# Casts in rows of 2 KB, rope tables loaded a unit ahead, and wide softmax sums, in an encoder layer on eight cores

## The chip, the cores and the metric

The kernel runs on the 8 cores of one Trainium2 chip, every core on its own half of one of the four batch items' queries. The metric is the device time of the slowest core, in microseconds (us). Engines are named as the profile names them: PE is TensorE (its weight loads, PEld, lie beside the matmuls), DVE is VectorE, ACT is ScalarE, POOL is GpSimd, SP is SyncE, which here only starts transfers.

An execution can fall in a slow state, in which one die's cores get a lower clock and the program takes some per cent longer.

## The reference, cut to what matters

```python
# per layer, x: (4, 4096, 2048) float32
qa, ka, va, qb, kb, vb, ga, gb = jnp.split(x @ w_in, split_pts, axis=-1)
qa = rope(rms_norm(qa))          # A: 8 query heads, 2 key heads, full softmax over 4096 keys
ka = rope(rms_norm(ka))
out_a = softmax(qa @ ka.T * scale) @ va
out_b = dilated_window_attention(qb, kb, vb)     # B: 12 heads in 3 groups of dilation 1, 4, 16
mixed = (sigmoid(ga + b0) * (out_a @ w_proj_a) + sigmoid(gb + b1) * (out_b @ w_proj_b)) @ w_out
x = layer_norm(ALPHA * x + mixed)
x = layer_norm(ALPHA * x + (silu(x @ w_ffn_gate) * (x @ w_ffn_up)) @ w_ffn_down)
```

The weights come as float32; the matmuls run in bfloat16. So each weight is cast once, either on its way into SBUF or, for out-projection and feed-forward weights that are read several times, from DRAM to a bfloat16 copy in DRAM.

## The kernel before

Instructions are recorded by a helper `s` that works out semaphores from the buffers read (`r`) and written (`w`); so in a profile nearly all matmuls carry one line number (L223), all two-input VectorE and GpSimd operations another (L232), and one reads by buffer names. SP starts loads and stores on the hardware queue (q1 in the profile). GpSimd starts transfers that cast, on the software queue (q0).

The casts of the later weights are a list of jobs, taken one or two at a time at chosen places of the program. Each is one transfer of 1 or 2 MB (counted as written), whose rows are 4 to 16 KB long.

```python
    jobs = []
    for j in range(22):
        jobs.append((wgb_d[j], w_fg_d[j], ("wgb", j)))
        jobs.append((wub_d[j], w_fu_d[j], ("wub", j)))
        jobs.append((wdb_d[j * 256:(j + 1) * 256, :], w_fd_d[j * 256:(j + 1) * 256, :], ("wdb", j)))
    for fb in range(4):
        jobs.append((wob_d[fb], w_out_d[fb], ("wob", fb)))
    jobs.reverse()
    ...
    def precast(n=1):
        for _ in range(min(n, len(jobs))):
            out, in_, key = jobs.pop()
            s.dma("pool", DMA(out, in_), w=[key])
```

The table of cosines and sines for 512 positions (512 KB) is loaded when the unit that needs it begins. There are two buffers:

```python
    def load_cs(tb):
        i = n_cs[0] % 2
        n_cs[0] += 1
        s.dma("sp", DMA(CS[i][:, :, :], rope_d[tb]), w=[(CS[i],)])
        return i
```

In `rope`, VectorE multiplies the projection by this table (R1, R2), and then makes SQL, the low half of the squares, which TensorE sums with a matrix of ones. That is why a late table shows up as TensorE waiting for SQL.

Attention A goes through 512 steps: 8 heads, 4 blocks of 512 queries, 16 steps of 256 keys. A group is the 16 steps of one head and block. A step is two score matmuls into one of three double banks, an exp on ScalarE (PT), and three steps later (LAG) two value matmuls. The sums of the softmax are built from pairs on VectorE and accumulated in float32 on GpSimd:

```python
            j = i - LAG
            if 0 <= j < len(steps):
                h, qb, pc = steps[j]
                g = h // 4
                p, q = PT[j % 6], PS[j % 6]
                s.dve(TT(q[:, :], p[:, 0:512], p[:, 512:1024], ALU.add), r=[(p,)], w=[(q,)])
                if pc % 2 == 1:
                    q0 = PS[(j - 1) % 6]
                    s.dve(TT(q[:, :], q[:, :], q0[:, :], ALU.add), r=[(q,), (q0,)], w=[(q,)])
                if pc == 3:
                    q1 = PS[(j - 2) % 6]
                    s.pool(TT(DAC[:, :], q[:, :], q1[:, :], ALU.add), r=[(q,), (q1,)], w=[(DAC,)])
                elif pc % 2 == 1 and pc > 3:
                    s.pool(TT(DAC[:, :], DAC[:, :], q[:, :], ALU.add), r=[(q,), (DAC,)], w=[(DAC,)])
                # ... value matmuls of step j into bank 6 ...
                if pc == 15:
                    ou = OU[(h * 4 + qb) % 2]
                    s.dve(CP(ou[:, :], psb[6][:, :]), w=[(ou,)], ps=[6])
                    s.pool(CP(DHI[:, :], DAC[:, :]), r=[(DAC,)], w=[(DHI,)])
                    s.pool(TT(DLO[:, :], DAC[:, :], DHI[:, :], ALU.subtract), r=[(DAC,), (DHI,)], w=[(DLO,)])
                    due.append((i + 5, h, qb))
            if due and i >= due[0][0]:
                # ... two ones-products (DHI, DLO) into bank 7 sum over the partitions ...
                s.dve(CP(rd[:, :], psb[7][:, :]), w=[(rd,)], ps=[7])
                s.dve(RECIP(rd[:, :], rd[:, :]), r=[(rd,)], w=[(rd,)])
                s.dve(TT(oa[:, :], ou[:, :], rd[:, :], ALU.mult), r=[(rd,), (ou,)], w=[(oa,)])
                s.dma("sp", DMA(oaT_d[h][:, qb * 512:(qb + 1) * 512], oa[:, :]), r=[(oa,)], w=[("oaT", h, qb)])
```

Between these steps TensorE also does the gate and projection of out_b ("fill"), whose results go to DRAM (mb). The keys of B (kbT) and queries of B are projected partly before and partly within attention B: each 512-column piece goes through one of four staging buffers STG to DRAM, and attention B loads them into KB and QB.

The softmax here doesn't subtract the row's maximum and nothing guards it: scores larger than these inputs give would overflow.

Of the kernel before, what the change touches and what calls it, by code (L numbers as in the profile page):

```python
# [5 lines left out]
F32 = mybir.dt.float32  # L6
# [275 lines left out]
def build_program():  # L282
# [86 lines left out]
    jobs = []  # L369
    for j in range(22):  # L370
        jobs.append((wgb_d[j], w_fg_d[j], ("wgb", j)))
        jobs.append((wub_d[j], w_fu_d[j], ("wub", j)))
        jobs.append((wdb_d[j * 256:(j + 1) * 256, :], w_fd_d[j * 256:(j + 1) * 256, :], ("wdb", j)))
    for fb in range(4):
        jobs.append((wob_d[fb], w_out_d[fb], ("wob", fb)))
# [88 lines left out]

    def load_cs(tb):
        i = n_cs[0] % 2
        n_cs[0] += 1
        s.dma("sp", DMA(CS[i][:, :, :], rope_d[tb]), w=[(CS[i],)])
        return i
# [147 lines left out]
    def vb_rest():  # L617
        load_r(5)
        for g in (1, 2):
            for i in range(2 if g == 1 else 0, B_TILES[g]):  # L620
                vb_tile(g, i)
                if i % 4 == 3:
                    precast()
                yield
            if g == 1:
                load_r(7)
        for i in range(6, 12):
            load_r(i + 3)
            for _ in kq_units(i, P1):
                yield  # L630
            precast(2)
# [155 lines left out]
    def kq_rest():  # L787
        for i in range(12, 18):
            load_r(i + 3)
            yield from kq_units(i, FB)  # L790
            precast(2)
# [24 lines left out]
    PT = [at("PT", [128, 1024], BF16, kb(120 + 2 * i)) for i in range(6)]  # L816
    PS = [at("PS", [128, 512], BF16, kb(132 + i)) for i in range(6)]
    DAC = at("DAC", [128, 512], F32, kb(138))
    DHI = at("DHI", [128, 512], BF16, kb(140))
    DLO = at("DLO", [128, 512], BF16, kb(141))  # L820
    RD = [at("RD", [128, 512], F32, kb(142 + 2 * i)) for i in range(2)]
    OU = [at("OU", [128, 512], F32, kb(146 + 2 * i)) for i in range(2)]
    OA = [at("OA", [128, 512], BF16, kb(150 + i)) for i in range(2)]
    OB = at("outbT", [128, 4, T], BF16, kb(96))
    MBL = [at("MBL", [128, T], F32, kb(152 + 8 * i)) for i in range(3)]
# [5 lines left out]
    FILL = {9: 2, 10: 1, 11: 2, 12: 1, 13: 2, 14: 2, 15: 1, 0: 2, 1: 1, 2: 2, 4: 2, 5: 2}  # L831

    def attn_a(fill):
# [3 lines left out]
        due = []  # L837
        load_kv(1)
        for i in range(len(steps) + LAG + 16):
            if i < len(steps):  # L840
                h, qb, pc = steps[i]
                g = h // 4
                if qb == 0 and pc == 0 and h + 1 < 8:
                    load_q(h + 1)
                bk = i % 3
                for e2 in range(2):
                    c = 2 * pc + e2
                    kf = FRAG[g * 4 + c // 8]
                    s.pe(MM(pbig[bk][:, e2 * 512:(e2 + 1) * 512], kf[:, (c % 8) * 128:(c % 8 + 1) * 128],
                            QT[h % 2][:, qb * 512:(qb + 1) * 512]),  # L850
                         r=[(kf,), (QT[h % 2],)], ps=[2 * bk + e2])
                s.act(ACTF(PT[i % 6][:, :], pbig[bk][:, :], AF.Exp), w=[(PT[i % 6],)], ps=[2 * bk, 2 * bk + 1])
# [6 lines left out]
            for _ in range(FILL.get(i % 16, 0) if i >= 16 + 9 else 0):  # L859
                next(fill, None)  # L860
            j = i - LAG
            if 0 <= j < len(steps):
                h, qb, pc = steps[j]
                g = h // 4
                p, q = PT[j % 6], PS[j % 6]
                s.dve(TT(q[:, :], p[:, 0:512], p[:, 512:1024], ALU.add), r=[(p,)], w=[(q,)])
                if pc % 2 == 1:
                    q0 = PS[(j - 1) % 6]
                    s.dve(TT(q[:, :], q[:, :], q0[:, :], ALU.add), r=[(q,), (q0,)], w=[(q,)])
                if pc == 3:  # L870
                    q1 = PS[(j - 2) % 6]
                    s.pool(TT(DAC[:, :], q[:, :], q1[:, :], ALU.add), r=[(q,), (q1,)], w=[(DAC,)])
                elif pc % 2 == 1 and pc > 3:
                    s.pool(TT(DAC[:, :], DAC[:, :], q[:, :], ALU.add), r=[(q,), (DAC,)], w=[(DAC,)])
                for jj in ((), (j - 1, j), (j,))[min(pc, 2)]:
                    pp = PT[jj % 6]
                    for e2 in range(2):
                        c = 2 * (jj % 16) + e2
                        vf = FRAG[8 + g * 4 + c // 8]
                        s.pe(MM(psb[6][:, :], vf[:, (c % 8) * 128:(c % 8 + 1) * 128], pp[:, e2 * 512:(e2 + 1) * 512],  # L880
                                start=(c == 0), stop=(c == 31)),
                             r=[(vf,), (pp,)], ps=[6])
                if pc == 15:
                    ou = OU[(h * 4 + qb) % 2]
                    s.dve(CP(ou[:, :], psb[6][:, :]), w=[(ou,)], ps=[6])
                    s.pool(CP(DHI[:, :], DAC[:, :]), r=[(DAC,)], w=[(DHI,)])
                    s.pool(TT(DLO[:, :], DAC[:, :], DHI[:, :], ALU.subtract), r=[(DAC,), (DHI,)], w=[(DLO,)])
                    due.append((i + 5, h, qb))
            if due and i >= due[0][0]:
                assert i % 16 == 7  # L890
                _, h, qb = due.pop(0)
                n = h * 4 + qb
                ou, oa, rd = OU[n % 2], OA[n % 2], RD[n % 2]
                s.pe(MM(psb[7][:, :], ones_b[:, :], DHI[:, :], start=True, stop=False), r=[(DHI,)], ps=[7])
                s.pe(MM(psb[7][:, :], ones_b[:, :], DLO[:, :], start=False, stop=True), r=[(DLO,)], ps=[7])
# [49 lines left out]
    def mb_fill():  # L945
        for f in range(NMB):
            for tb in range(4):
                t, st = TG[tb % 2], TG[2 + tb % 2]
                for kc, _ in enumerate(gate(f, 1, tb, 7)):
                    if kc == 15:  # L950
                        tanh(f, 1, 7, t)
                        precast(1 + (n_jobs() > NMB * 4 - f * 4 - tb))
# [6 lines left out]
            if f < 3:  # L959
                load_mb(f)  # L960
# [15 lines left out]
    load_oa(range(4, 8))  # L976
    MIX = [at("mixT", [128, T], BF16, kb(112 + 4 * f)) for f in range(16)]
# [28 lines left out]
    for f in range(16):  # L1006
# [8 lines left out]
        elif f == 14:  # L1015
            WO0A = at("WO0A", [128, 8, 512], BF16, kb(176))
            s.dma("sp", DMA(WO0A[:, :, :], wob_d[0][:, 0:4096].rearrange("p (k c) -> p k c", c=512)),
                  r=[("wob", 0)], w=[(WO0A,)])
# [15 lines left out]
    def load_wo(fb):  # L1034
        s.dma("sp", DMA(WO[fb][:, :, :], wob_d[fb].rearrange("p (k c) -> p k c", c=512)), r=[("wob", fb)], w=[(WO[fb],)])
# [58 lines left out]
    def next_bank():  # L1094
# [4 lines left out]
          r=[("wob", 0)], w=[(WO0B,)])  # L1099
# [42 lines left out]
    def ensure_gu(upto):  # L1142
        while gu_next[0] <= upto and gu_next[0] < 88:
# [3 lines left out]
            s.dma("sp", DMA(t[:, 0, :], wgb_d[i % 22]), r=[("wgb", i % 22)], w=[(t, 0)])  # L1147
            s.dma("sp", DMA(t[:, 1, :], wub_d[i % 22]), r=[("wub", i % 22)], w=[(t, 1)])

    def ensure_d(upto):  # L1150
        while d_next[0] <= upto and d_next[0] < 7 * NHC:
# [6 lines left out]
                  r=[("wdb", hc // 2)], w=[(t,)])  # L1158
# [60 lines left out]
    for tb in range(4):  # L1219
# [31 lines left out]
        for half in range(2):  # L1251
# [13 lines left out]
            for hc in range(NHC - 4):  # L1265
                ensure_d(d0 + hc + 7)
                if tb == 3:
                    t = WDL[hc]
                    s.dma("sp", DMA(t[:, :], wdb_d[hc * 128:(hc + 1) * 128, 1024:2048]), r=[("wdb", hc // 2)], w=[(t,)])
# [17 lines left out]
    for i, hc in enumerate(range(NHC - 4, NHC)):  # L1287
        t = WD[i]
        s.dma("sp", DMA(t[:, :], wdb_d[hc * 128:(hc + 1) * 128, 1024:2048]), r=[("wdb", hc // 2)], w=[(t,)])
# [117 lines left out]
```

## Time and profile before

Three runs took 4632 to 4638 us, and the cores agree within 1%. The stages below are read off TensorE's timeline at the first matmul of each kind (core 1, the slowest).

| stage | what it is | us |
|---|---|---|
| keys/values | keys and values of A, first value tiles of B | 289.9 |
| queries and keys | queries of A, value tiles of B; then keys and queries of B | 597.6 |
| attention B | first to last; other keys and queries of B woven in | 394.5 |
| attention A | first score matmul to last | 747.0 |
| to out-projection | the end of attention A and the mixing | 505.9 |
| rest | out-projection, norms, feed-forward | 2104.3 |

How to read it: a stage is worth shortening only by what TensorE stands still in it.

### The profile page before, as it was taken

How to read it: one execution, taken by the hardware profiler on the slowest of the kernel's cores; microseconds unless marked ns; L12 is line 12 of the kernel's file. 1: busy time of each engine (PE TensorE's matmuls, PEld its weight loads, DVE VectorE, ACT ScalarE, POOL GpSimd, SP SyncE). 2: the span in 40 equal slices, each digit the busy share in tenths (PEclk: the TensorE clock that was granted, in tenths of full speed). 3: DMA queues.
4: the chain of work that ended last, by engine and by line, in shares of the span. 5: the costliest groups of instructions: out<-in, count | busy, mean ns of one | idle time of the engine just before them, and what ended most of it. 6: DMA issues, size and time to landing. Idle time of an engine off the chain costs nothing.

```text
span 4639.1 us, 55832 instructions; the slowest of 8 cores (4603.6 to 4639.1 us)
## 1 busy us (share of the span) xinstructions
PE 4172.2 (90%) x19488; PEld 1930.7 (42%) x19488; DVE 1589.8 (34%) x2127; ACT 1079.1 (23%) x1432; POOL 448.1 (10%) x523
## 2 busy tenths in 40 slices
PE   6678598859788888879999999999999999999998
PEld 3333254324433333334444444444444444444443
DVE  1224230013688989962222661000220022012203
ACT  1223121112376666641111221000110011001100
POOL 2000000000034444420000000000000000000000
PEclk9889799989789999989999999999999999999999
DMA  9665748692455444363222456455455644554463
GB/s 158 107 97 91 110 84 136 136 150 103 159 102 94 97 96 84 64 112 92 45 38 83 174 179 212 170 176 166 169 198 166 178 173 178 170 170 170 175 191 111
DMA packets 233970, 622.24 MB, mean 134 GB/s; under 512 B 55328, under 2 KB 110624, under 8 KB 200224
## 3 DMA queue, kind: packets, MB, share of 16 engines
q1 hardware_dynamic: 197808, 476.01, 31.7%
q0 software_dynamic: 35888, 142.65, 21.0%
q8 instruction: 162, 2.65, 0.2%
q14 instruction: 112, 0.92, 0.1%
HBM read 676.61 MB, written 162.20 MB: 181 GB/s over the span
## 4 chain that ended last, share of the span: by engine, by line
PE 74%; DMA 11%; DVE 9%; issue 3%; ACT 2%; another core or an unknown queue 1%; SPq 0%; DVEq 0%; POOL 0%; ACTq 0%; POOLq 0%
PE pbig L223 74%; DMA CS_58<-rope 3%; DMA CS_57<-rope 2%; DMA kbT<-STG_78 2%; DMA qbT<-STG_79 1%; DVE PS_128 L232 1%; DVE PS_126 L232 1%; DVE PS_124 L232 1%; DMA kbT<-STG_79 1%; DVE RD_133 L249 1%; DVE RD_132 L249 1%; DMA kvw_54<-w_in_t 1%; DMA oat_158<-oaT 1%; DVE R_25_67 L240 0%
## 5 line engine op out<-in xcount | busy, mean ns | idle before, releaser
L223 PE MATMUL pbig<-xT_52,ring_56 128*128 128x512 bf16 (+2 forms) x1792 | 390.9, 377 | 52.0 <-ACT STG_79 L229 34.1
L223 PEld LDWEIGHTS pbig<-xT_52,ring_56 128*128 128x128 bf16 x1792 | 172.9, 100 | 253.2 <-issue 71.6
L229 ACT ACTIVATE SGL_206<-pbig 128x512 f32<-128x512 f32 x88 | 52.6, 598 | 932.5 <-PE pbig L223 932.3
L223 PE MATMUL pbig<-xT_52,WM_143 128*128 128x512 bf16 x1024 | 250.2, 381 | 1.0 <-DVE RD_133 L243 0.9
L223 PE MATMUL pbig<-xT_52,WM_142 128*128 128x512 bf16 x1024 | 250.4, 379 | 0.2 <-DVE RD_133 L243 0.2
L232 DVE TENSOR_TENSOR HT_197<-SGL_207,pbig 128x512 bf16<-128x512 f32 x88 | 60.5, 688 | 503.4 <-PE pbig L223 503.4
L232 DVE TENSOR_TENSOR HT_197<-SGL_206,pbig 128x512 bf16<-128x512 f32 x88 | 60.4, 687 | 479.9 <-PE pbig L223 475.8
L223 PE MATMUL pbig<-X1T_193,WGU_196 128*128 128x512 bf16 x960 | 209.6, 379 | 1.8 <-ACT XTS_190 L246 1.8
L223 PE MATMUL pbig<-X1T_193,WGU_194 128*128 128x512 bf16 x960 | 209.6, 379 | 1.7 <-ACT small_50 L229 1.7
L223 PE MATMUL pbig<-ring_56,xT_52 128*128 128x512 bf16 x944 | 209.8, 379 | 0.0
L223 PE MATMUL pbig<-X1T_219,WGU_195 128*128 128x512 bf16 x960 | 209.6, 379 | 0.0
L223 PE MATMUL pbig<-X1T_219,WGU_194 128*128 128x512 bf16 x960 | 209.6, 379 | 0.0
L223 PE MATMUL pbig<-X1T_193,WGU_195 128*128 128x512 bf16 x896 | 197.2, 381 | 3.4 <-DMA WGU_195<-wgb 3.4
L223 PE MATMUL pbig<-X1T_219,WGU_196 128*128 128x512 bf16 x896 | 195.7, 379 | 0.0
L229 ACT ACTIVATE SGL_207<-pbig 128x512 f32<-128x512 f32 x88 | 52.6, 598 | 513.7 <-PE pbig L223 513.7
L223 PEld LDWEIGHTS pbig<-xT_52,WM_143 128*128 128x128 bf16 x1024 | 100.3, 98 | 123.3 <-issue 4.4
L223 PEld LDWEIGHTS pbig<-ring_56,xT_52 128*128 128x128 bf16 x944 | 114.0, 121 | 90.1 <-issue 0.2
L223 PEld LDWEIGHTS pbig<-xT_52,WM_142 128*128 128x128 bf16 x1024 | 100.0, 98 | 121.5 <-issue 1.4
L223 PE MATMUL pbig<-SQL_63,ones_b_44 128*128 128x512 bf16 x24 | 10.9, 456 | 147.7 <-DVE SQL_63 L232 147.5
L223 PEld LDWEIGHTS pbig<-X1T_193,WGU_196 128*128 128x128 bf16 x960 | 93.8, 98 | 115.0 <-issue 1.9
L223 PEld LDWEIGHTS pbig<-X1T_193,WGU_194 128*128 128x128 bf16 x960 | 93.9, 98 | 114.9 <-issue 1.9
L223 PEld LDWEIGHTS pbig<-X1T_219,WGU_195 128*128 128x128 bf16 x960 | 93.9, 98 | 113.3
(697 smaller groups left out, 6709.2 us busy)
## 6 DMA issues: line engine op xcount, KB each, us to landing
WGU_194<-wgb SPq DMA_DIRECT2D x30, 1024.0 KB, 4.9
WGU_194<-wub SPq DMA_DIRECT2D x30, 1024.0 KB, 5.1
WGU_195<-wgb SPq DMA_DIRECT2D x29, 1024.0 KB, 4.9
WGU_195<-wub SPq DMA_DIRECT2D x29, 1024.0 KB, 4.9
WGU_196<-wgb SPq DMA_DIRECT2D x29, 1024.0 KB, 4.9
WGU_196<-wub SPq DMA_DIRECT2D x29, 1024.0 KB, 5.0
wgb<-w_fg_t POOLq DMA_DIRECT2D x22, 1024.0 KB, 19.0
wub<-w_fu_t POOLq DMA_DIRECT2D x22, 1024.0 KB, 17.6
```

Of the source, the lines that this page charges most:

```text
L223: return lambda e: e.matmul(out, lhsT=lhsT, rhs=rhs, start=start, stop=stop, **kw)
L229: return lambda e: e.activation(out=out, in_=in_, func=func, **kw)
L232: return lambda e: e.tensor_tensor(out=out, in0=in0, in1=in1, op=op)
L249: return lambda e: e.reciprocal(out=out, in_=in_)
```

## The change

Its intent is to take four kinds of waits away: VectorE's adds that GpSimd slows, rope tables that arrive late, and stores and loads that stand behind long packets of the casts. Cut to its core:

```diff
+    def add_jobs(out, in_, name):
+        for c in range(0, out.shape[1], 1024):
+            jobs.append((out[:, c:c + 1024], in_[:, c:c + 1024], name + (c // 1024,)))
     for j in range(22):
-        jobs.append((wgb_d[j], w_fg_d[j], ("wgb", j)))
+        add_jobs(wgb_d[j], w_fg_d[j], ("wgb", j))
     ... (the same for wub, wdb and wob; the readers wait for the pieces they need; precast calls are spread out)
     def load_cs(tb):
-        i = n_cs[0] % 2
+        n = n_cs[0]
         n_cs[0] += 1
-        s.dma("sp", DMA(CS[i][:, :, :], rope_d[tb]), w=[(CS[i],)])
-        return i
+        for m in ((0, 1) if n == 0 else (n + 1,)):
+            if m < len(cs_order):
+                s.dma("sp", DMA(CS[m % 2][:, :, :], rope_d[cs_order[m]]), w=[(CS[m % 2],)])
+        return n % 2
     ... (attention A: PT has 8 slots in one buffer, P2 and six P4 buffers; the fill stands at other steps, two loads of mb come later)
-                s.dve(TT(q[:, :], p[:, 0:512], p[:, 512:1024], ALU.add), r=[(p,)], w=[(q,)])
-                ... (second add, all GpSimd work)
+                if pc % 4 == 3:
+                    a = (j - 3) % 8
+                    p4 = P4[(j // 4) % 6]
+                    s.dve(TT(P2[:, :].rearrange("p (a b) -> p a b", a=2), PT[:, a:a + 2, :], PT[:, a + 2:a + 4, :],
+                             ALU.add), r=[(PT, a + k) for k in range(4)], w=[(P2,)])
+                    s.dve(TT(p4[:, :], P2[:, 0:1024], P2[:, 1024:2048], ALU.add), r=[(P2,)], w=[(p4,)])
     ... (after the group, in two consecutive steps)
-                s.pe(MM(psb[7][:, :], ones_b[:, :], DHI[:, :], start=True, stop=False), r=[(DHI,)], ps=[7])
-                s.pe(MM(psb[7][:, :], ones_b[:, :], DLO[:, :], start=False, stop=True), r=[(DLO,)], ps=[7])
+                for k in (2 * late, 2 * late + 1):
+                    p4 = P4[(n * 4 + k) % 6]
+                    for e2 in range(2):
+                        s.pe(MM(psb[7][:, :], ones_b[:, :], p4[:, e2 * 512:(e2 + 1) * 512],
+                                start=(k == 0 and e2 == 0), stop=(k == 3 and e2 == 1)), r=[(p4,)], ps=[7])
```

## The prediction

> **What bounds the kernel now.** I read the views in this order: spans of all cores, busy time by stage, what TensorE (PE) waited for in each stage, the groups of the stage that waits most, and the DMA queues in the stretches where a wait ended in a DMA. All cores agree (4604 to 4639 us, granted clock 0.95), so core 1 stands for all. I found the stage borders in TensorE's timeline. Columns: stretch, length, then busy us (instructions) of PE, weight loads, VectorE (DVE), ScalarE (ACT), GpSimd (POOL), then granted clock, DMA share, GB/s.
>
> ```profile
> 0.00:289.90 289.90, 200.54 (x1102) 112.46 (x1103) 66.11 (x100) 58.65 (x114) 40.77 (x71) 0.89 0.74 118
> 289.90:637.00 347.10, 248.67 (x1088) 124.30 (x1089) 128.10 (x186) 86.84 (x156) 16.87 (x33) 0.85 0.61 102
> 637.00:887.50 250.50, 218.56 (x1029) 105.30 (x1028) 5.27 (x8) 39.53 (x70) 22.20 (x43) 0.93 0.73 122
> 887.50:1285.00 397.50, 309.82 (x1625) 161.80 (x1623) 152.31 (x177) 96.85 (x132) 11.04 (x22) 0.84 0.58 137
> 1285.00:2046.00 761.00, 652.54 (x2735) 270.87 (x2735) 675.33 (x929) 519.67 (x551) 345.57 (x334) 0.93 0.50 91
> ...
> 2821.00:4639.00 1818.00, 1797.01 (x8320) 813.50 (x8320) 282.20 (x370) 140.06 (x214) 0.00 (x0) 1.00 0.51 171
> ```
>
> The stages are: keys and values of A; queries of A mixed with value tiles of B; keys and queries of B; attention B; attention A; and last the feed-forward stage, which is TensorE at full clock and which the change doesn't touch. There the chain of waits has 374.86 us for 1736 matmuls, so a warm 128x512 matmul costs 0.216 us. With that price attention A's 2735 matmuls need 591 us; it takes 761. The four stages before it also stand still a good deal. What for:
>
> ```profile
> PE pbig L223 <- DVE SQL_63 L232: 57.3, 4, 16.1
> ...
> PE pbig L223 <- DVE SQL_63 L232: 90.2, 6, 41.9
> ...
> PE pbig L223 <- ACT STG_79 L229: 18.3, 1, 18.3
> PE pbig L223 <- ACT STG_78 L229: 13.7, 2, 8.3
> ...
> PE pbig L223 <- DMA KB_85<-kbT: 35.5, 3, 33.7
> ...
> PE pbig L223 <- DVE OU_134 L243: 36.4, 16, 3.6
> ```
>
> These are total us, times, longest, stage by stage. The first two end in VectorE, but VectorE itself was waiting for the rope tables: in the first 560 us it waited 263 us in 12 waits for the two table buffers. SQL is only the third piece of work behind the table in VectorE's order. The STG waits are ScalarE waiting for a 128 KB store to leave its staging buffer (up to 26.6 us), so they too are DMA. Why a transfer of 512 KB is late, from the DMA view of 455 to 560 us:
>
> ```profile
> q0 software_dynamic: 2016, 9.44, 75.1%
> q1 hardware_dynamic: 2892, 3.17, 10.4%
> ...
> wub<-w_fu_t POOLq DMA_DIRECT2D x2, 1024.0 KB, 47.9
> ...
> CS_58<-rope SPq DMA_DIRECT2D x1, 512.0 KB, 49.1
> ```
>
> The casts' queue holds the engines: 0.751 x 105 us x 16 engines / 2016 packets = 0.63 us per packet of 4.7 KB on average, against 0.06 us per packet of the hardware queue. The table lands when the casts have drained.
>
> Attention A in its groups (count; busy us, mean ns; idle before):
>
> ```profile
> L232 DVE TENSOR_TENSOR PS_124<-PT_118 128x512 bf16<-128x512 bf16 x86 | 89.1, 1036 | 0.0
> L229 ACT ACTIVATE PT_118<-pbig 128x1024 bf16<-128x1024 f32 x86 | 88.1, 1025 | 58.2 <-PE pbig L223 28.5 <-DVE PS_124 L232 23.5 <-DVE PS_126 L232 5.6
> L232 POOL TENSOR_TENSOR DAC_129<-DAC_129,PS_126 128x512 f32<-128x512 f32 x64 | 75.4, 1178 | 108.4 <-DVE PS_126 L232 96.4 <-DVE PS_127 L232 6.4 <-PE pbig L223 5.5
> L249 DVE RECIPROCAL RD_133<-RD_133 128x512 f32<-128x512 f32 x16 | 53.6, 3352 | 1.6
> L232 DVE TENSOR_TENSOR PS_127<-PT_121 128x512 bf16<-128x512 bf16 x85 | 43.9, 516 | 0.0
> ```
>
> The same 512-wide bf16 add takes 1.04 us in one group and 0.52 in another. The timeline shows why:
>
> ```profile
> 1603.75 0.42 DVE L232 TENSOR_TENSOR PS_127<-PT_121 128x512 bf16<-128x512 bf16 x1
> ...
> 1603.98 1.21 POOL L232 TENSOR_TENSOR DAC_129<-DAC_129,PS_126 128x512 f32<-128x512 f32 x1 [5.23 <-DVE PS_126 L232]
> ...
> 1604.09 1.38 DVE L232 TENSOR_TENSOR PS_128<-PT_122 128x512 bf16<-128x512 bf16 x1
> ```
>
> Alone the add takes 0.42 us (one every 0.34); beside a GpSimd add it takes 1.38. So VectorE, 675 of 761 us busy and seldom idle, bounds this stage, and a third of its time is GpSimd's doing. It is late with the copy OU that frees the one accumulation bank: TensorE stands about 2 us per group of 16 steps (67 us in all), 29 us more for a tanh, and the gaps leave it at half clock for some us (matmuls 0.43 us apart around 1616 us).
>
> **What the skill says.** GPSIMD Engine Reference, Specifications: its SBUF interfaces are shared with VectorE, in contention with VectorE instructions that have two SBUF inputs. The trace agrees (0.42 against 1.38 us). VectorE: DVE Perf Modes, The perf-mode tier table: a bf16 tensor_tensor of 2048 elements takes 1224 ns; 0.42 us at 512 fits a fixed 0.15 us plus 2 elements per cycle. DMA: Bandwidth & Descriptors, Queues, rings and completion order: each engine goes round its queues packet by packet, so long packets of one queue delay the other. The shares above agree in direction. TensorE: Matmul & The Clock Gate, Part 1: half clock after an idle window of about 3.4 us. The trace shows 0.43 against 0.216 us after shorter gaps too.
>
> **Attention A, part by part.** The unit is a group of 16 steps (one head, 512 queries), 32 of them; one takes 23.65 us (from 1427.15 to 1450.80).
> VectorE loses 24 adds of 512 and gains 4 of 2048 and 4 of 1024. Start to start, less the 0.08 us of overlap seen in the timeline, I estimate 1.14 and 0.61 us: 4 x 1.75 = 7.0 us. The old adds cost 8 x 1.04 + 16 x 0.51 = 16.5. What stays: copies 0.68 and 0.69, reciprocal 3.35, product 0.69, fill 0.69 = 6.1. New sum 13.1 us.
> GpSimd loses all its adds, casts and subtractions (7 x 1.17 + 0.71 + 1.15 = 10 us) and keeps DMA issues, so the 1.38 us adds go.
> ScalarE: 16 exps about 0.93 us apart and a tanh: 15.5 us, as before.
> TensorE loses 2 ones-products and gains 8: 32 + 32 + 20 + 8 = 92 matmuls x 0.2155 = 19.8 us instead of 86 x 0.2155 = 18.5. It becomes the bound. The 6 extra are 32 x 6 x 0.2155 = 41 us of real new work, paid only because 5.1 us of standstill per group goes.
> The slack: 5 matmuls (1.08 us) lie between the last product and the next use of the bank, for a copy of 0.68 us that now finds VectorE free; 9 (1.94 us) between the tanh's input and its use, against some 1.9 needed. After the reciprocal the next wide add is about 2 us late; three steps of score banks absorb that. I allow 0.4 us per group: 20.2 x 32 = 647 us. Gain 114.
>
> **Rope tables.** The load of the next table now stands a whole unit ahead, about 13.8 us of TensorE work plus some 7 us until the first ones-product needs it. Latencies seen were 13 to 24 us, and 42 to 49 in the worst cast burst. Keys and values: 57.3 us of waits, of which I expect 48 to go, with 8 us of slow clock after them (32 matmuls took 5.0 to 6.2 instead of 3.7 us): 56. Queries: 90.2 us; the burst after the third weight load (9 MB) stays, so I expect 65 plus 10 of slow clock: 75.
>
> **Casts in 2 KB rows.** 296 transfers of 256 KB instead of 70, the same bytes. The new calls are spread in program order, but GpSimd runs ahead of TensorE and issues them in the same bursts; what shrinks is the packet. An 8 KB packet costs some 1 to 1.5 us, a weight-load packet 0.2 to 0.3; I take 0.3. A store or load then passes 3 to 4 times sooner. Keys and queries of B: 32 us of STG waits, 26 go, 3 of clock: 29. Attention B: 38 us for KB and 20 for STG; the burst of 8 MB (966 to 1047 us) stays as bytes, so I count 38 plus 5: 43. After attention A TensorE waits 12 us for out_a behind a 2 MB cast: 8 go. Issue time on GpSimd, 226 x 0.5 us more, lies on an idle engine.
> MBL 1 and 2 load later, but 28 us before use.
>
> **Sum.** 114 + 56 + 75 + 29 + 43 + 8 = 325; 4638 - 325 = 4313, say **4310 us**.
>
> **Rivals.** (1) The early stages turn from waiting for tables to waiting for DMA altogether: prefetched or not, tables and stores share one hardware queue, and a query unit has an estimated 56 packets per engine (tables 8, queries 16, values 32) in 13.8 us, while a saturated casts' queue lets one pass per 0.36 us: 20 us. Store or staging waits would take the tables' place. For it: DMA share 0.6 to 0.74 and 91% casts' queue at 966 to 1047 us. Against: saturation lasts only tens of us. It would take 80 us of gain: 4390. (2) In attention A the reciprocal's 3.35 us, or TensorE's own extra work, eats more: 1.5 us per group more gives 4360. (3) Everything hides: all table, STG and KB waits and the half-clock time go: 4240. (4) More descriptors make casts slower and starve weight loads: 4400; the ring's 30 loads of 4 KB source rows land in 9.7 us, which speaks against.
>
> **Range and chances.** Rivals 1 and 3 set the ends: 4240 to 4385. Within 2% needs a loss of two thirds of the sum, though attention A alone is worth 2.5%: faster 0.96, same 0.035, slower 0.005.
>
> **What would show it.** Attention A near 650 us with TensorE near 98% at clock 0.99, VectorE near 420 us busy, the 2048-wide add near 1.2 us, no GpSimd adds; if the add takes 2 us or more, the contention has another source. VectorE's waits for CS near 40 us instead of 283. kbT stores landing below 10 us even in bursts. The stages from mixing on unchanged within 10 us but for the wait before mixing. I am wrong if stores or STG waits grow in the query stage, or if weight loads (ring, WM) appear among TensorE's waits.

## The result, and the profile after

On one chip the kernel before took 4632 to 4638 us in four runs. The changed kernel took 4376.1 and 4367.3 us in its two fast runs (two more: 4753 and 4837, with one die at clock 0.87 to 0.89). The ratio is 0.9432, with a 95% interval of 0.9409 to 0.9454. A ratio is the mean time of one kernel's fast runs over that of the other's of the same rounds, so it isn't quite the ratio of the medians. The gain is about 264 us; 325 had been counted.

The stretches of core 4, the slowest of the changed kernel, in the columns of the prediction's first fence (stretch, length, busy us and instructions of PE, weight loads, DVE, ACT, POOL, then granted clock, DMA share, GB/s):

```profile
0.00:236.50 236.50, 195.88 (x1102) 110.25 (x1102) 66.10 (x100) 57.66 (x114) 40.00 (x70) 0.97 0.90 146
236.50:498.60 262.10, 245.90 (x1088) 124.13 (x1089) 129.14 (x186) 86.51 (x156) 33.18 (x64) 0.95 0.81 133
498.60:710.70 212.10, 212.10 (x1028) 103.92 (x1027) 4.84 (x7) 39.11 (x68) 44.72 (x87) 1.00 0.92 136
710.70:1113.30 402.60, 311.19 (x1618) 160.78 (x1617) 150.48 (x175) 95.39 (x131) 34.34 (x67) 0.85 0.79 150
1113.30:1790.00 676.70, 645.90 (x2942) 280.03 (x2940) 435.83 (x421) 515.43 (x553) 78.03 (x153) 1.00 0.72 98
```

The third stretch has no standstill left: 212.10 us busy of 212.10. The fifth has its clock back (1.00 from 0.93), and VectorE is busy for 436 us instead of 675. The fourth stands out: it has the same clock and the same busy time as before, and a DMA share of 0.79 instead of 0.58. By stages:

| stage | before (core 1) | after (core 4) | difference | predicted |
|---|---|---|---|---|
| keys/values | 289.9 | 236.6 | -53 | -56 |
| queries and keys | 597.6 | 474.1 | -124 | -104 |
| attention B | 394.5 | 402.6 | +8 | -43 |
| attention A, scores | 747.0 | 662.2 | -85 | -114 |
| to out-projection | 505.9 | 485.2 | -21 | -8 |
| rest | 2104.3 | 2113.9 | +10 | 0 |

Cores differ in some of these rows for reasons outside the change: the query-and-key stage of the kernel before took 562 us on core 4; attention B took 394 to 400 us over the eight cores before and 393 to 403 after, so its +8 is no loss, only no gain; and the rest ran between 2100 and 2114 us on the cores of these two kernels. By the means of all eight cores the six differences are -54, -106, +1, -84, -20 and +4. The rows to explain are the first four.

What TensorE waits for up to the end of the mixing in the changed kernel (total us, times, longest):

```profile
PE pbig L223 <- DMA KB_85<-kbT: 26.7, 5, 7.7
PE pbig L223 <- ACT PT_117 L229: 24.7, 36, 1.7
...
PE pbig L223 <- DMA KB_84<-kbT: 20.8, 3, 8.6
PE pbig L223 <- DVE SQL_63 L232: 17.5, 5, 5.7
```

The SQL wait, 147.5 us in all before, is 17.5: the tables are there. VectorE's own waits for them in the first 560 us, in the kernel before (first two lines) and in one of the two buffers of the changed one (the other, CS_58, had 4.5 us):

```profile
DVE R_23_65 L240 <- DMA CS_58<-rope: 133.2, 6, 50.0
DVE R_23_65 L240 <- DMA CS_57<-rope: 130.0, 6, 49.6
...
DVE R_23_65 L240 <- DMA CS_57<-rope: 8.5, 2, 4.3
```

Of the OU and TG waits of attention A, 96 us before, 4 are left; a new one, for the exp PT, has come. The KB waits were one long one and a few short (38 us); now they are eight of up to 8.6 us, and 47.5 us in all.

In attention A, the costliest group of VectorE (count; busy us, mean ns; idle before):

```profile
L232 DVE TENSOR_TENSOR P_76_118<-PT_117 128x2048 bf16<-128x2048 bf16 x128 | 156.1, 1220 | 5.6 <-ACT PT_117 L229 1.1 <-DVE P_80_122 L232 0.9 <-DVE P_78_120 L232 0.9
```

The wide add takes 1.22 us, as the prediction took it. Its name P_76 stands for the one buffer P2.

### The profile page after: what moved, and what is told of

It is laid out like the page before. It is cut to its first block, busy times and chain, and to the rows that moved or that the text cites. A ratio compares the mean times of both kernels' runs of the same rounds, so it can differ in the third digit from the quotient of the medians.

```text
span 4374.6 us, 54216 instructions; the slowest of 8 cores (4346.0 to 4374.6 us)
## 1 busy us (share of the span) xinstructions
PE 4151.9 (95%) x19680; PEld 1934.3 (44%) x19680; DVE 1348.2 (31%) x1615; ACT 1070.6 (24%) x1432; POOL 241.9 (6%) x461
## 4 chain that ended last, share of the span: by engine, by line
PE 80%; DMA 10%; DVE 5%; ACT 2%; issue 2%; SPq 0%; POOL 0%; DVEq 0%; ACTq 0%; another core or an unknown queue 0%; POOLq 0%
PE pbig L223 80%; DMA kbT<-STG_78 1%; DVE RD_125 L249 1%; DVE RD_126 L249 1%; DMA BIAS_94<-bbias 1%; DVE P_76_118 L232 1%; DMA qbT<-STG_78 1%; DMA qaT<-QST_71 1%; ACT PT_117 L229 1%; DMA qbT<-STG_79 1%; DMA kvw_54<-w_in_t 1%; DMA WO_177<-wob 1%; DMA CS_57<-rope 1%; DMA KB_85<-kbT 0%; DMA KB_84<-kbT 0%
## 5 line engine op out<-in xcount | busy, mean ns | idle before, releaser
L229 ACT ACTIVATE PT_117<-pbig 128x1024 bf16<-128x1024 f32 x512 | 493.0, 1032 | 154.4 <-DVE P_76_118 L232 92.1
L223 PEld LDWEIGHTS pbig<-xT_52,ring_56 128*128 128x128 bf16 x1792 | 172.4, 100 | 216.4 <-issue 34.5
L232 DVE TENSOR_TENSOR P_76_118<-PT_117 128x2048 bf16<-128x2048 bf16 x128 | 156.1, 1220 | 5.6 <-ACT PT_117 L229 1.1
L223 PEld LDWEIGHTS pbig<-ring_56,xT_52 128*128 128x128 bf16 x944 | 114.7, 122 | 96.2 <-issue 8.5
L223 PEld LDWEIGHTS pbig<-xT_52,WM_134 128*128 128x128 bf16 x1024 | 100.0, 98 | 122.1 <-issue 1.4
L223 PEld LDWEIGHTS pbig<-xT_52,WM_133 128*128 128x128 bf16 x1024 | 100.0, 98 | 121.0
L223 PEld LDWEIGHTS pbig<-X1T_186,WGU_187 128*128 128x128 bf16 x960 | 93.8, 98 | 115.1 <-issue 2.0
L223 PEld LDWEIGHTS pbig<-X1T_186,WGU_189 128*128 128x128 bf16 x960 | 93.8, 98 | 114.9 <-issue 1.8
```

The lines of the kernel that those rows point to most:

```text
L223: return lambda e: e.matmul(out, lhsT=lhsT, rhs=rhs, start=start, stop=stop, **kw)
L229: return lambda e: e.activation(out=out, in_=in_, func=func, **kw)
L232: return lambda e: e.tensor_tensor(out=out, in0=in0, in1=in1, op=op)
```

## The experiments

All ran as eight-core kernels with results that agree with the reference. Times are of fast runs; the kernel before had medians of 4624 to 4626 us, its few slow runs included, in the rounds beside them. The columns are the stages of the table above, on the slowest core of the profiled run except where another core is named; a few us between two such entries can be the cores' own spread.

| run | fast runs, us | ratio to before | keys/values | queries, keys | att. B | att. A | to out-proj. |
|---|---|---|---|---|---|---|---|
| changed kernel | 4367, 4376 | 0.943 | 236.6 | 474.1 | 402.6 | 662.2 | 485.2 |
| e1 long casts | 4513 to 4543 | 0.977 | 236.2 | 549.8 | 395.0 | 741.1 | 486.6 |
| e2 no lead | 4485 to 4506 | 0.971 | 289.1 | 558.1 | 402.6 | 662.2 | 485.3 |
| e3 old attention | 4482, 4484 | none given | 232.4 | 487.2 | 407.8 | 751.0 | 492.5 |
| e4 late reciprocal (core 1) | 4336, 4390 | 0.943 | 232.2 | 473.8 | 392.2 | 638.5 | 485.2 |
| e5 GpSimd adds | 4380 to 4395 | 0.949 | 237.0 | 482.1 | 394.3 | 677.4 | 486.9 |
| e6 no casts in B | 4307 to 4318 | 0.933 | 236.8 | 480.3 | 343.6 | 664.2 | 486.7 |
| e7 e4 and e6 (core 0) | 4287 to 4315 | 0.930 | 234.2 | 469.9 | 343.5 | 636.9 | 485.2 |
| e8 rows of 4 KB | 4437 to 4462 | 0.963 | 239.4 | 526.8 | 404.1 | 675.7 | 486.9 |
| e9 rows of 1 KB | 4331 to 4347 | 0.938 | 232.9 | 460.9 | 383.1 | 661.9 | 486.7 |
| e10 e7, more casts moved | 4298 to 4305 | 0.930 | 238.2 | 460.3 | 344.1 | 637.1 | 514.1 |
| e11 e7 and e9 | 4267 to 4280 | 0.923 | 234.4 | 464.8 | 340.5 | 636.5 | 485.1 |

### e1: the change without its short casts

```diff
-            jobs.append((out[:, c:c + 1024], in_[:, c:c + 1024], ...))   # and all calls that go with it
+        jobs.append((wgb_d[j], w_fg_d[j], ("wgb", j)))                   # as in the kernel before
```

> The changed kernel with the weight casts put back to long rows (8 KB and more) and their old places; rope tables a unit ahead and the new attention A stay. Theory P (packet length matters): table loads behind a burst land up to 49 us late against a lead of about 20 us, so the query stage (262 us) gets 30 to 50 us longer, the key and query stage of B (212 us) gets its 30 us of STG waits back, attention B keeps some 400 us: about 4440 us in all. Rival Q (the lead does it all, short rows only cost DMA time, their queue took 1142 us of 16 engines instead of 974): stages of queries and keys within 10 us, attention B 30 to 40 us shorter because the casts' queue is done sooner: about 4340 us.

The calls stand at their old places again too, so row length, transfer size and spreading went back together. The fast runs took 4513 to 4543 us, some 150 us above the changed kernel and further than either theory put it. Half of the loss is in the query and key stages (549.8 against 474.1 us), where tables and stores stand behind long packets again. The other half was in nobody's sum: attention A went back from 662.2 to 741.1 us (726 to 743 over the cores), close to its length in the kernel before. TensorE's waits in attention A of this run:

```profile
PE pbig L223 <- DMA outbT<-obT: 41.9, 2, 31.8
PE pbig L223 <- ACT PT L229: 36.9, 35, 12.8
PE pbig L223 <- DVE TG L240: 19.9, 1, 19.9
```

The loads of out_b that the fill needs took 56 us to land at the median (8 in the kernel before, 32 in the changed one), and a store of a TG buffer held TensorE for another 20 us. These are single stalls: the first group took 65.5 us and two near the end 42.3 and 34.4, while nearly all others took some 20.7 us, as in the changed kernel. So the new softmax sums and the short casts depend on each other: with long casts the wide adds bring attention A 6 us on the slowest core, with short ones 85.

The traces show why those loads landed within 8 us in the kernel before, with the same casts. Here are the first casts of attention A and the loads of out_b, in the kernel before and in e1:

```profile
1297.52 9.95 SPq L226 DMA_DIRECT2D outbT_138<-obT  x16
...
1332.51 0.53 POOL L226 DMA_DIRECT2D wub<-w_fu_t  x1
...
1194.17 0.51 POOL L226 DMA_DIRECT2D wub<-w_fu_t  x1
...
1197.02 23.58 SPq L226 DMA_DIRECT2D outbT<-obT  x8
```

In the kernel before GpSimd had 15 adds, copies and subtractions of the softmax sums to do before it reached its first cast, 35 us after the loads had gone out. Without them it reached its casts before the loads, and issued eight casts in 4 us, 8 MB. So taking GpSimd's work away also took away what had paced its transfers; the prediction saw only that GpSimd's lane would be idle. e5, which puts adds back, agrees: there the first cast goes out 26 us after the loads, and these land in 3.1 us instead of 32. No run changes the issue order alone. Attention B, on the other hand, wasn't longer at all (395.0 against 402.6 us).

### e2: the change without the lead of the tables

```diff
-        for m in ((0, 1) if n == 0 else (n + 1,)):
-            ...
+        s.dma("sp", DMA(CS[i][:, :, :], rope_d[tb]), w=[(CS[i],)])
```

> The changed kernel with the rope tables loaded at the start of their own unit again; short casts and new attention A stay. Theory P: in the first stage the loads that hold the engines are x and weights, which the change leaves alone, so its 57 us of waits come back whole (236 to 290 us); in the query stage a table behind short packets lands in 10 to 25 us instead of 24 to 49, so about half of the 90 us comes back (262 to 305 us): about 4470 us. Rival R (short packets alone make tables come in time): both stages within 15 us of the changed kernel, about 4385 us.

It took 4485 to 4506 us, about 120 above the changed kernel, and the loss is where it should be: 52 us in keys/values, 84 in queries and keys on this core, none from attention B on. VectorE's wait in the first 560 us:

```profile
DVE R L240 <- DMA CS<-rope: 286.8, 14, 51.0
```

With the lead, the two table buffers cost VectorE 13 us there. This run has short casts and its VectorE still waits as long as in the kernel before. In keys/values the tables alone made the stage late (e1, with long casts, stays at 236.2 us). In queries and keys both count: of the 106 us gained by the means of all cores, e2 loses 68 and e1 62.

### e3: the change with the old attention A

```diff
-                if pc % 4 == 3:
-                    ... (wide adds, eight ones-products)
+                s.dve(TT(q[:, :], p[:, 0:512], p[:, 512:1024], ALU.add), r=[(p,)], w=[(q,)])
+                ... (as in the kernel before, GpSimd's work included)
```

> The changed kernel with attention A as before (narrow adds, GpSimd sums, MBL early); short casts and tables ahead stay. If the parts are independent, attention A takes 768 us again instead of 678 and nothing else moves: 4371 + 90 = 4461 us, and VectorE adds of 512 again split into 0.42 and 1.38 us. If the gain of attention A came partly from the casts (their GpSimd issues and DMA share there rose from 0.50 to 0.72), attention A takes over 780 us here.

Two runs were fast, 4482 and 4484 us, some 111 above the changed kernel; two were slow, and no ratio was given. Attention A took 751.0 us, as in the kernel before (747.0), so short casts alone bring nothing there: VectorE was its bound, not DMA. The early stages kept their gains.

The three losses are 152, 122 and 111 us by the means of the fast runs, 386 in all, and the whole change gained 264. Most of the excess is attention A's: its 79 to 89 us are lost when either of two parts is taken away, and so they are counted twice.

### e4: the reciprocal two steps later

In the changed kernel a group takes 20.68 us on average and 20.73 at the median (four of the reciprocals start at 1187.44, 1208.18, 1228.87 and 1249.60 us), and TensorE has 92 matmuls in it, 92 x 0.2155 = 19.83 us. So 0.85 us per group is lost. The timeline of the changed kernel shows where (start, us, engine, operation; in brackets the idle time before and its releaser):

```profile
1228.87 3.35 DVE L249 RECIPROCAL RD_125<-RD_125 128x512 f32<-128x512 f32 x1
...
1232.33 0.69 DVE L232 TENSOR_TENSOR OA_129<-OU_127,RD_125 128x512 bf16<-128x512 f32 x1
...
1232.93 1.22 DVE L232 TENSOR_TENSOR P_76_118<-PT_117 128x2048 bf16<-128x2048 bf16 x1
...
1234.36 2.85 ACT L229 ACTIVATE PT_117<-pbig 128x1024 bf16<-128x1024 f32 x3 [3.00 <-DVE P_76_118 L232]
...
1235.52 0.59 PE L223 MATMUL pbig<-QT_116,frag_102 128*128 128x512 bf16 x2 [0.65 <-ACT PT_117 L229]
```

The wide add stands behind the reciprocal and the product in VectorE's order. ScalarE can't overwrite its eight exp slots until the add has read them, stands 3.00 us, and TensorE feels the last 0.65 us of it. The experiment issues the reciprocal, the product and the store two steps later, after the wide add that used to stand behind them:

```diff
                 s.dve(CP(rd[:, :], psb[7][:, :]), w=[(rd,)], ps=[7])
+                rest_of.append((i + 2, h, qb))
+            if rest_of and i >= rest_of[0][0]:
+                _, h, qb = rest_of.pop(0)
+                ...
                 s.dve(RECIP(rd[:, :], rd[:, :]), r=[(rd,)], w=[(rd,)])
```

> The changed kernel with the reciprocal and the product after it issued two steps later, behind the next pair of wide adds, with the same work. In the changed kernel ScalarE waits 3.0 us per group of 16 steps for the wide add that stands behind the 3.35 us reciprocal, and TensorE then waits 0.65 us; a group takes 20.7 us against 19.8 of matmuls. Theory S (that order is the cause of what attention A lacks against 647 us): TensorE's waits for PT fall from 19 us to under 5, a group takes 19.9 to 20.1 us, attention A 678 to about 655 us, total 4348 us. Rival: TensorE is limited by matmul issue itself and the wait merely moves: within 5 us of the changed kernel.

Attention A took 638.5 us instead of 662.2, and a group 19.92 us at the median, 0.09 us above its matmuls' 19.83. ScalarE's waits for the wide add between 1150 and 1740 us, 86 us in 30 waits of up to 3.4 in the changed kernel, in this run:

```profile
ACT PT L229 <- DVE P L232: 14.1, 33, 0.8
```

The whole kernel's ratio (0.9426, interval 0.9337 to 0.9514) can't show these 24 us, because in one of the two fast runs, the profiled one, the median core of one die was 41 us longer than that of the other (4369 against 4328; core 1 is of the other); the run in which both dies agreed took 4336 us. The stage length shows it, on every core read.

### e5: needless GpSimd adds beside the wide adds

The prediction put a third of VectorE's old time down to GpSimd, from one look at the timeline. Here eight float32 adds per group go back to GpSimd, with a result that nobody reads:

```diff
+                if pc % 2 == 1:
+                    s.pool(TT(DAC[:, :], DAC[:, :], PT[:, j % 8, 0:512], ALU.add), r=[(PT, j % 8), (DAC,)], w=[(DAC,)])
```

> The changed kernel, with 8 needless float32 adds of 512 put back on GpSimd in each group of attention A (running sum in one scratch buffer, one exp half as second operand, result unused, output still right). Theory (GpSimd slows VectorE's two-input adds, as the timeline of the kernel before suggested with 0.42 against 1.38 us): the 2048-wide add, 1.22 us in the changed kernel, becomes 1.8 us or more on average, because four of the eight GpSimd adds start together with a wide add; VectorE's busy time in the stage goes from 431 to above 500 us, ScalarE waits longer for the wide add, and attention A grows from 678 to between 700 and 740 us: 4400 to 4435. Rival (the narrow adds of before were slow by their own form): the wide add stays at 1.22 us and the time at 4375.

VectorE's groups in attention A of this run:

```profile
L232 DVE TENSOR_TENSOR P<-PT 128x2048 bf16<-128x2048 bf16 x126 | 177.6, 1410 | 4.5 <-DVE P L232 2.1 <-issue 0.3
L232 DVE TENSOR_TENSOR P<-P 128x1024 bf16<-128x1024 bf16 x126 | 147.4, 1170 | 14.0 <-DVE P L232 1.3
L249 DVE RECIPROCAL RD<-RD 128x512 f32<-128x512 f32 x31 | 103.9, 3353 | 3.5 <-DVE RD L243 0.5
```

The narrower of the two adds went from 0.69 to 1.17 us and the wide one from 1.22 to 1.41, while the reciprocal, which has one input, stayed at the 3353 ns that it has in the changed kernel. So the contention is real and hits two-input adds, as the Trainium skill says (GPSIMD Engine Reference, Specifications). VectorE's busy time rose to 525 us. But the wide add gained 0.19 us where I expected 0.6 or more, and attention A grew by 15 us where I expected 22 to 62: VectorE is no longer the bound, and most of its delay seems to be slack (ScalarE waited only 4 us for GpSimd itself). The time, 4380 to 4395 us, lies between the theory's 4400 to 4435 and the rival's 4375. The direction is shown; its size in the kernel before, where VectorE was full, isn't measured by this.

### e6: no casts in attention B

The KB waits of attention B didn't shrink with short casts. In the trace of the changed kernel the DMA engines are full from about 530 to 955 us. In the first part of attention B, 711 to 955 us, the queues stood like this (packets, MB, share of 16 engines):

```profile
q0 software_dynamic: 11527, 20.97, 73.7%
q1 hardware_dynamic: 10111, 17.41, 26.7%
```

That sums to the whole: a KB load, which must follow a store of the same keys, waits for 12 us of store and 14 us of load. The casts put more on the stage than before: over the whole of it their queue (weight loads included) moved 21.05 MB in 44.8% of the engines' time, against 15.73 MB in 29.5% in the kernel before. The experiment takes away what fills the queue. The 56 casts issued within attention B go to the mixing stage, whose DMA share is 0.28:

```diff
     def kq_rest():
...
-            for n, c in enumerate(kq_units(i, FB)):
-                if n % 4 == 3:
-                    precast()
-                yield c
+            yield from kq_units(i, FB)
...
             load_wm(f + 2, 1)
+            precast(4)
```

(The out-projection's weights move to the head of the list, and attention A leaves 56 jobs over.)

> The changed kernel, with the 56 casts issued during attention B moved to the mixing stage (whose DMA share is 0.28), and out-projection weights first in the list. Theory S (the casts' queue is saturated until the middle of attention B, and each KB load, which must follow a store of the same keys, then takes 12 + 14 us): attention B loses the 47 us of KB waits and most of the 13 us of STG waits, from 403 to about 355 us, KB loads land below 9 us again, and the kernel takes about 4330. Rival F (the order in which the keys of B are woven into attention B makes KB late, whatever the queue does): KB waits stay above 35 us, attention B at 390 or more, 4365. If the casts disturb the mixing stage, its 455 us grow or weight loads show among TensorE's waits.

Attention B took 343.6 us instead of 402.6 and the kernel 4307 to 4318 us. Attention B of this run in the view by stretches, and its KB waits:

```profile
717.20:1060.70 343.50, 299.20 (x1617) 159.12 (x1616) 150.30 (x175) 95.78 (x131) 5.66 (x11) 0.88 0.47 134
```

```profile
PE pbig L223 <- DMA KB<-kbT: 13.5, 4, 6.2
```

The stores of keys land in 2.1 us at the median instead of 12. The mixing stage kept its length. Theory S stands, and rival F, the order of the weaving, accounts for no more than the 13.5 us left.

### e7: e6 and e4 together

> The run before and the late reciprocal together. The two act in different stages, so the gains should add: attention A 654 instead of 678 us, attention B 355 instead of 403: about 4295. If attention B keeps its length (rival F): 4335.

The edit is the sum of the two. Attention B took 343.5 us and attention A 636.9, and the fast runs 4287, 4293 and 4315 us. (The last is the profiled one, where the slowest core, core 4, spent 491.5 us in queries and keys; core 0 stands in the table as one without that.) The gains add; this version beats both kernels.

### e8: rows of 4 KB

```diff
-        for c in range(0, out.shape[1], 1024):
-            jobs.append((out[:, c:c + 1024], in_[:, c:c + 1024], name + (c // 1024,)))
+        for c in range(0, out.shape[1], 2048):
+            jobs.append((out[:, c:c + 2048], in_[:, c:c + 2048], name + (c // 2048,)))
```

(Half as many precast calls, and readers that name the larger pieces.) The edit doesn't quite do what its name says. The rows of the down weights (wdb) are only 4 KB long, so their blocks are whole again: the trace has 704 packets of 32 KB, 23.1 MB, which is all of wdb. The other casts, 54.5 MB, move in packets of 4 KB.

> The changed kernel with casts in rows of 4 KB: half the transfers, half the packets, the same bytes. Theory S (in attention B the engine time of the casts counts, 141 us of one engine per MB in rows of 2 KB against 105 in long rows): the queue is drained sooner, attention B is 10 to 20 us shorter, the stages before it unchanged, 4355. Rival L (the length of the packet counts everywhere, as it did with the long casts, which cost 50 to 75 us in the query and key stages and 75 us in attention A): stores and the loads of out_b take longer, roughly a third of the long casts' loss: 4420.

It took 4437 to 4462 us, on rival L's side. But as 30% of the bytes kept the packets of the long casts, it isn't shown how much of the loss the packets of 4 KB account for. The query and key stages took 526.8 us, between the 474.1 of rows of 2 KB and the 549.8 of long rows. Attention B didn't change (404.1), with KB waits as long as ever:

```profile
PE pbig L223 <- DMA KB<-kbT: 47.3, 6, 20.8
```

### e9: rows of 1 KB

```diff
-        for c in range(0, out.shape[1], 1024):
+        for c in range(0, out.shape[1], 512):
```

> The changed kernel with casts in rows of 1 KB: twice the transfers and packets, the same bytes. Rule L alone (the shorter the packet, the less everything else waits: 4519 with the long rows, 4448 with 4 KB, 4372 with 2 KB) would go on to about 4340. Rival T (short packets cost engine time: in attention A 97 us of one engine per MB in rows of 4 KB, 141 in rows of 2 KB, so a fixed part of some 0.11 us per packet and, for 1 KB, an estimated 195 per MB): attention A's DMA share rises from 0.72 to about 0.95, the casts' queue never drains, weight loads or loads of out_b appear among TensorE's waits, and the kernel takes 4400 or more. I expect T.

I expected theory T, and it fell: 4331 to 4347 us in the three fast runs, where rule L alone put 4340. The gain lies in queries and keys (460.9 us against 474.1) and in attention B (368 to 383 us over the cores, against 393 to 403). The queue of the casts during attention A, in this run:

```profile
q0 software_dynamic: 41651, 42.38, 65.7%
```

That is 0.657 x 660 us x 16 / 41651 = 0.167 us per packet, 164 us of one engine per MB instead of the 195 estimated, and a DMA share of 0.82 instead of 0.95. The error lay in taking a packet's time for work. (The figure for 4 KB rows was mixed besides, with e8's packets of 32 KB in it.) In this run's stage of keys and queries the shares sum to more than there is:

```profile
500.00:711.00 211.00, 211.00 (x1052) 100.94 (x1051) 5.72 (x7) 40.97 (x69) 81.91 (x159) 1.00 1.02 141
```

A share of 1.02 can only be had if packet times overlap or hold waiting. They show which queue is in another's way, but extrapolating them to a new size doesn't work. TensorE's busy time in that stage is full all the same.

### e10: the query stage's casts moved as well

```diff
-                if i % 2 == 1:
-                    precast(2)
...
-            precast(4)
+            precast(7)
```

> The version with the late reciprocal and without casts in attention B, and the 40 casts of the query stage moved to the mixing stage too (96 there, 7 per feature block). If the casts of the query stage still make rope tables late (21 us of TensorE waits there), the stage shrinks from 262 to 271 us to about 245, and the kernel takes 4275 against 4287 to 4314 of the version it grew from. If those waits come from the query weights' own loads, nothing changes there. If the mixing stage can't hold 96 casts (an estimated DMA share of 0.65), its weight loads become late and its 455 us grow.

The query and key stages shrank to 460.3 us (469.9 in e7), as the first theory had it, and the mixing stage grew from 455.8 to 483.6, with a wait that it had not had:

```profile
PE pbig L223 <- DMA WM<-w_mix_t: 19.7, 4, 7.8
```

Weights for the mixing share the casts' queue, and seven casts ahead of a weight load were too many. The times, 4298 to 4305 us, are those of e7: a gain that was given back.

### e11: rows of 1 KB, no casts in attention B, the late reciprocal

> All that helped, together: rows of 1 KB, no casts in attention B (112 short ones in the mixing stage, 8 per feature block), the late reciprocal. If the gains add: up to attention B about 690 us as with rows of 1 KB, attention B 343, attention A 637, mixing 456: about 4270, against 4287 to 4314 without the shorter rows. If 8 short casts per block make the mixing stage's weights late, as 7 casts of twice the length did (475 to 484 instead of 456), the stage grows and 4290 is left.

Eight casts per feature block, each half as long as e10's, didn't disturb the mixing stage (455.8 us). Four runs, all fast, took 4267 to 4280 us, a ratio of 0.9233 (0.9158 to 0.9309). The stages of attention B, attention A and mixing:

```profile
699.20:1039.70 340.50, 298.15 (x1617) 158.69 (x1616) 150.16 (x175) 95.01 (x130) 5.72 (x11) 0.89 0.49 133
1039.70:1691.00 651.30, 641.37 (x2943) 282.54 (x2942) 430.44 (x421) 531.53 (x553) 151.76 (x297) 1.00 0.78 102
1691.00:2146.00 455.00, 455.00 (x2109) 206.29 (x2109) 106.75 (x155) 63.22 (x92) 69.11 (x134) 1.00 0.56 93
```

In attention A and mixing together, TensorE stands still for 10 us in 1106. This is the best version.

## Why the prediction was right or wrong

**The total** was right: the range was 4240 to 4385 us, and both fast runs, 4367 and 4376, lie in it, near its upper end. Of the 325 us summed, 264 came. The mechanisms of the two largest terms held, attention A and the tables; but the sum also missed a term of 79 us that happened to be granted, and that part was luck. Step by step:

- **Rope tables: right.** Keys/values lost 53 us (56 predicted). VectorE waits 13 us for tables instead of 263 (40 predicted), and e2 gives the first stage back whole, and 68 of 106 us of the second, when the lead alone is taken away. Queries and keys together lost 124 us on the slowest cores, or 88 if core 4 is compared with core 4; 104 had been predicted, so the term is right within what the cores differ. Of the store waits that rival 1 feared in the query stage, VectorE had 18 us for its staging buffer of queries (QST), and TensorE felt next to nothing of it.
- **Casts, keys and queries of B: right.** TensorE is busy in every microsecond of it. e1, with all the casts long, and e8, with some, lose time there.
- **Casts, attention B: wrong, and this is the largest miss.** "The burst of 8 MB (966 to 1047 us) stays as bytes, so I count 38 plus 5: 43." The stage gained nothing (393 to 403 us over the cores, against 394 to 400). The step took the one wait of 33.7 us for the effect of packet length and the burst for an episode of 80 us, and the bytes weren't the same (14.7 MB against 12.6). In the changed kernel the queue is full for 425 us, and each KB load comes after a store, 26 us in all; e1, e8 and e9 show KB waits of 44, 47 and 37 us with long rows, 4 KB and 1 KB. Rows of 1 KB took some 20 us off the stage (e9); taking the casts away took 59 (e6, 54 by the means of all cores, with 13.5 us of KB waits left). "Saturation lasts only tens of us", said against rival 1, was wrong in the same way; rival 1 was right in kind, but in the stage after the one it named.
- **"kbT stores landing below 10 us even in bursts": wrong.** They took 10 to 12 us by buffer at the median, in a stage whose first part is saturated.
- **"An 8 KB packet costs some 1 to 1.5 us": wrong.** In the trace of the kernel before the casts move in 2368 packets of 32 KB, which took 3.3 us at the median (2.4 to 5.0 between the tenth and ninetieth percentile). The rows of the gate and up weights are 8 KB long, but the blocks are whole; the average of 4.7 KB came from mixing the casts with smaller packets. In the changed kernel the casts move in packets of 2 KB, and packets of that size on their queue took 0.17 us at the median and 0.28 on average (0.3 had been taken). So the change cut the packets by sixteen.
- **Attention A: the mechanism was right, the allowance for slack too small.** VectorE's 436 us (420 predicted), the add's 1.22 us, TensorE's 92 matmuls per group and the clock of 1.00 are as predicted. The term that failed is "I allow 0.4 us per group": it was 0.85. "After the reciprocal the next wide add is about 2 us late; three steps of score banks absorb that" overlooked the exp slots: there are eight, a wide add reads four of them, and it is issued only two steps before ScalarE needs the first again. e4 shows it: 0.8 us per group at the median, 24 us of the stage, come back by moving one instruction. Of the 29 us that attention A fell short, some 5 remain; they weren't traced.
- **A term was missing.** The short casts were counted for 80 us in three places, and attention A wasn't among them. e1 shows that without them attention A would have been 79 us longer, from loads of out_b and stores behind long packets. The sum contained this only because it assumed it: it took TensorE to be the next bound after VectorE, without asking what DMA would allow at the new pace, nor what GpSimd would issue earlier once its adds were gone.
- **The wait before mixing: right in direction.** 8 us had been counted; the stage lost 21, of which the wait for out_a was 11 and waits for GpSimd's last sums 6.5 (e3, with the old sums, stays some 6 us above the changed kernel). The wait for out_a didn't come back with the long casts (e1: 486.6 us), so the step's reason, a 2 MB cast ahead of the load, isn't confirmed.
- **Rival 4, more descriptors make casts slower: wrong up to rows of 1 KB.** No weight load of the ring or of the mixing became late, save in e10.

Two things stay open: the cost of GpSimd's adds in the kernel before, as e5 measures it only where VectorE has slack; and whether it is the length of a packet or the size of a transfer that counts, as the two were always halved or doubled together.

## What to carry to other kernels

Where a background transfer shares engines with stores and loads that the compute waits for, cut its rows short to protect single transfers, but first ask whether the queue is full for longer than the wait: then moving the bytes to a stage with an idle DMA helps most (54 to 59 us here, against some 20 for rows half as long). Before an engine is relieved of work, look at what it issues after that work, because the work may have paced it. When an engine stops being the bound, walk through every buffer of the loop and count the steps between its last reader and its next writer, because the new slack is the smallest of them. Long instructions that nobody waits for, such as a reciprocal, belong behind the short ones that somebody does wait for.

## What the Trainium skill lacked or had wrong

- DMA: Bandwidth & Descriptors, Bandwidth: its rule is to batch transfers to 1 MiB and more. For transfers in the background of others the opposite held here: whole casts of 1 to 2 MB (packets of 32 KB) gave 4513 to 4543 us, e8's mix of packets of 4 and 32 KB 4437 to 4462, 2 KB (256 KB each) 4367 and 4376, and 1 KB (128 KB each) 4331 to 4347. The rule is about a transfer's own bandwidth, which wasn't measured here; what a transfer costs its neighbours the page doesn't give.
- DMA: Bandwidth & Descriptors, Queues, rings and completion order: it says that an engine goes round its queues packet by packet, and the runs agree in direction; it gives no time for which a packet holds an engine. During attention A the casts' queue shows 0.283 and 0.167 us per packet for rows of 2 and 1 KB, and packets of 4 KB took 0.39 us on average in e8; these times hold waiting, since a stage's share reached 1.02.
- GPSIMD Engine Reference, Specifications: it names the contention with two-input VectorE instructions and gives no time for it. (The page SBUF — State Buffer says more of who blocks whom, which no run here tests.) Here a 1024-wide bf16 add went from 0.69 to 1.17 us and a 2048-wide one from 1.22 to 1.41 beside GpSimd's float32 adds; the reciprocal stayed at 3.35.
- VectorE: DVE Perf Modes, First, the fixed hardware budget: it tells that Reciprocal repeats its divide 8 times, and no duration. A 128x512 float32 reciprocal took 3.35 us, five times the 0.69 us of a copy of that size out of PSUM. The page's 1224 ns for a bf16 add of 2048 (The perf-mode tier table) agrees with the 1220 measured.
